# Earlier input rows at the start, and a new place for two output weight pieces and the mix rows, in a two-layer hybrid decoder trunk

## The chip, the cores and the metric

The kernel runs on one core of a Trainium2 chip. The metric is the time of one execution on the device in microseconds; the median of several runs is compared. Engines are called as in the profile: PE is TensorE's matmul, PEld its weight load, DVE is VectorE, ACT is ScalarE, POOL is GpSimd, SP is SyncE, which issues nearly all DMAs here (SPq in the rows).

## The reference

The input x is 2048 rows of 1024 float32. Two layers follow, each `x <- x + RMSNorm_post(mixer(RMSNorm_pre(x)))`. Cut to what matters:

```
def even_mixer(h, w_in, w_out):              # layer 0
    rq, rk, rv, rg, sq, sk, sv, sg = split_cols(h @ w_in, EVEN_SIZES)
    ret = rms_norm(retention(rq, rk, rv)) * silu(rg)        # 4 heads
    sb = stick_breaking(sq, sk, sv) * silu(sg)              # 8 heads
    return concat([ret, sb]) @ w_out                        # 1024 x 1024

def odd_mixer(h, w_in, w_out, ...):          # layer 1
    hq, hf, hi, hg, lx, lg = split_cols(h @ w_in, ODD_SIZES)
    hc = rms_norm(hgrn2(hq, hf, hi, lb)) * silu(hg)         # 4 heads, a gated recurrence
    hl = rg_lru(causal_conv(lx)) * silu(lg)                 # 512 channels, an associative scan
    return concat([hc, hl]) @ w_out                         # 1024 x 1024
```

## The kernel before, in words

The sequence is done in two halves of 1024 rows, so there are four rounds: layer 0 half 0, layer 0 half 1, layer 1 half 0, layer 1 half 1. A round is a mixer (`stick` for layer 0, `hgrn` for layer 1) followed by `out_phase`, the output projection, the post norm and the residual. While `out_phase` works, it also normalises and transposes the rows of the next round (`prep_rows`, `prep_cols`).

**Matmuls.** Every float32 operand of a large matmul is split into a high part (a rounded copy) and a low part (the remainder), and a product is three matmuls: high by high, high by low, low by high. `load_w` (lines 118 to 133) does this for weights: a DMA into a `raw` buffer (pool `wr`, two buffers of 4 KB a partition), a cast on ACT for the high part (L131), a subtraction on DVE for the low part (L132). `proj` (140) is one input projection: 128 output columns, two groups of 512 rows, 24 matmuls a group (L152). Its weights lie in pool `w`, two buffers.

**Start.** The identity for transposes and the two rows of `pre_norm_w` are loaded first (lines 50 to 54), then the eight rows of x of the first half (`row`, L94; a row here is a block of 128 rows) go through a square on ACT (L97), a reciprocal root on DVE and POOL (L70, L71) and a scaling on DVE (L99). After the fourth and the eighth row `step` (106) transposes a group on PE (L112) and makes its high and low part with `pre_norm_w` as a scale (L114 on ACT, L115 on DVE). The first two weight pieces are loaded behind rows 3 and 5 (L127).

**Layer 0.** `stick` opens nine pools, some 114 KB a partition, makes a constant `past` in PSUM from a scratch tile `build` (lines 375 to 379: memset, select on POOL, copy on ACT), and then weaves attention units with the projections and the retention. At its end `ret_gate` (287) projects the gates of heads 2 and 3 alone; each uses a 2 KB `sg` buffer of the two in pool `stmp` for a sigmoid (L296) that L297 reads. The retention's scratch (`srt`) lies behind them and is done earlier.

**Layer 1.** `hgrn` opens the recurrence's pools first (line 789): `lru1`, about 20 KB of scratch (a block-diagonal weight `bd` and four rows of 1024 elements), `lru5`, the four recurrence outputs `ht`, and `lrug`, one 2 KB gate tile `gt`. Behind them lie the pools of the four recurrent heads. `lx_proj(j)` fills `ht` j by a scan (L761); `lg_proj(j)` (769) projects the gates, multiplies by `ht` on POOL (on DVE for the last j; L777) and stores to DRAM, and the last j writes its part of the mix directly (`mix_direct`, L218 and L219). The last weave (934) runs the last head's scan beside the four `lg_proj`.

**Output projection.** `out_phase` (577) opens its pools over the mixer's: `w2` (four weight pieces with high and low part, 32 KB), `o2` (two buffers for rows of the mix), `o1` (post norm weights), `y` (results), then the next round's rows. A weight piece is two of the eight 128-row blocks of `w_out` by 512 columns (`piece`, 592); four pieces make the first 512 columns, four the second. `mix_rows` (221) loads 128 rows of the mix from DRAM (L225) and splits them into the buffers that held the mixer's input (L227 on ACT, L228 on DVE). PE then does 24 matmuls (L640) for each of eight row blocks, twice. `EARLY = (0, 1)` says how many mix row blocks are loaded ahead of `out_phase`, inside the last `lg_proj`, into a `raw` buffer (line 773): none in layer 0, one in layer 1.

**What sets the order.** The tile framework orders the instructions of each engine when the program is built, by the order of the text and its own estimate of when each is ready; each engine then runs its list in order. `tc.high_priority(offset=300)` moves a block 300 places ahead. Pools are stacked from the left end of SBUF, a pool with `side="right"` from the right end; a tile whose place was another tile's waits for that tile's last reader. `weave` and `mixed` interleave two generators by the times that they yield.

Of the kernel before, what the change touches and what calls it, by code (L numbers as in the profile page):

```python
# [9 lines left out]
F32 = mybir.dt.float32  # L10
# [3 lines left out]
ALU = mybir.AluOpType  # L14
# [8 lines left out]
EPS = 1e-6  # L23
LAG = 2
SHIFT = 1
EARLY = (0, 1)
LEVELS = (2, 4, 8, 16, 32, 64)


# [1 line left out]
def tile_trunk(ctx: ExitStack, tc: tile.TileContext, a: dict, out: bass.AP):  # L31
    nc = tc.nc
    x_in = a["x"][0]
    w_in = (a["even_w_in"][0], a["odd_w_in"][0])
    w_out = (a["even_w_out"][0], a["odd_w_out"][0])
# [4 lines left out]
    w_p = ctx.enter_context(tc.tile_pool(name="w", bufs=2))  # L40
# [7 lines left out]
        return (o_bank[-1] if tag == "o" else ps_p).tile([128, 512], F32, tag=tag, name=tag)  # L48

    ident = const.tile([128, 128], F32, name="ident")  # L50
    nc.sync.dma_start(out=ident, in_=a["c_ident"])
    pre_w = const.tile([128, 2, KD], F32, name="pre_w")
    for i in range(2):
        nc.sync.dma_start(out=pre_w[:, i, :], in_=a["pre_norm_w"][i].rearrange("(k p) -> p k", p=128))
    mhalf = const.tile([128, 4], F32, name="mhalf")
    nc.vector.memset(mhalf, -0.5)
    state = const.tile([128, 512], F32, name="state")
# [16 lines left out]
    def scope(es, name, bufs, **kw):  # L74
        return es.enter_context(tc.tile_pool(name=name, bufs=bufs, reuse_waits="tile", **kw))
# [61 lines left out]
    def proj_w(layer, col):  # L137
        ready[layer, col] = load_w(w_in[layer][:, col:col + 128], KD, 128)
# [54 lines left out]
    def weave(*args):  # L193
        run(mixed(*args))
# [175 lines left out]
    def stick(half, xT, M):  # L370
        with ExitStack() as es:
            kv_p, qr_p, q_p, a_p, b_p, wt_p, g_p, t_p, r_p = (scope(es, n, b) for n, b in (
                ("skv", 8), ("sqr", 2), ("sq", 2), ("sa", 6), ("sb", 9), ("swt", 3), ("sg", 3), ("stmp", 2), ("srt", 1)))
            past = scope_o(es, 1).tile([128, 512], F32, tag="past", name="past")
            build = t_p.tile([128, 512], F32, tag="sg", name="build")
            nc.vector.memset(build, 0.0)
            nc.gpsimd.affine_select(out=build[:, 384:512], in_=build[:, 384:512], compare_op=ALU.is_gt, fill=1.0,
                                    base=0, pattern=[[-1, 128]], channel_multiplier=1)
            nc.scalar.copy(out=past, in_=build)
            D_ = [({}, {}, {}, {}) for _ in range(4)]  # L380

            def pair_proj(pr):
# [169 lines left out]
            t_att = 65000 if half else 23000  # L552
            cs = rope_tables(half, r_p)
            run(pair_proj(0))
            flush()
            def qk(*parts):
                return ret_proj_qk(half, xT, r_p, t_p, cs, parts)
# [16 lines left out]
            weave(att(3), t_att, seq(side((5, 8), proj_of(1, pair_gate(3))), gate(0, 1)), 43500)  # L574
            run(gate(2, 3))

    def out_phase(layer, half, M, following):
        prep_row = prep_step = xT = None
        with ExitStack() as es:
            scope_o(es, 2)  # L580
            w2_p, p2, p1, y_p = scope(es, "w2", 4), scope(es, "o2", 2), scope(es, "o1", 1), scope(es, "y", 8)
            if following:
                rows, prep_row, x_p = prep_rows(es, *following)
                xT, prep_step = prep_cols(rows, following[0])
# [2 lines left out]
            early = EARLY[layer]  # L587
            mrs = [None] * early
            mh, ml = zip(*(mix_slot(M, g) for g in range(2)))
            order = (0, 1, 2, 4, 5, 6, 7, 3) if layer == 0 else tuple(range(8))  # L590

            def piece(c, q, pool):
                return load_w(w_out[layer][:, c * 512:(c + 1) * 512], 2, 512, pool, order[2 * q:2 * q + 2])

            with tc.high_priority(offset=300):
                W = [[piece(0, q, w2_p) for q in range(4)], []]
            with tc.high_priority(offset=300):
                for tt in range(early, 8):
                    mrs.append(mix_rows(half, M, tt, p2, "mr"))
# [25 lines left out]
            for c in range(2):  # L625
                if c == 1:
                    if not prep_step:
                        xrs.update((tt, load_x(tt)) for tt in range(8))
                    W[1] += [piece(1, q, w2_p) for q in (2, 3)]
                for tt in range(8):  # L630
                    if (c, tt) == (0, 2):
                        with tc.issue_after(mrs[5]):
                            W[1] += [piece(1, q, w_p) for q in (0, 1)]
# [150 lines left out]

        return lx_proj, lg_proj

    def hgrn(es, half, xT, M):
        scope_o(es, 2)
        lp1, lp5, lpg = scope(es, "lru1", 1), scope(es, "lru5", 4), scope(es, "lrug", 1)
        p1, p, p4 = scope(es, "hg1", 1), scope(es, "hg", 2), scope(es, "hg4", 4)  # L790
        ones = p1.tile([128, 128], F32, name="ones")
        nc.vector.memset(ones, 1.0)
# [138 lines left out]
        flush()  # L931
        for h in range(3):
            weave(head_scan(h), 20000, seq(head_proj(h + 1), lx_proj(h + 1)), 57000)
        weave(head_scan(3), 20000, seq(*(lg_proj(j) for j in range(4))), 41600)
        flush()

    steps = [(layer, half) for layer in range(2) for half in range(2)]
    with ExitStack() as es:
        rows, row, _ = prep_rows(es, 0, 0, 8)
        xT, step = prep_cols(rows, 0)  # L940
        for tt in range(8):
            row(tt)
            if tt in (3, 5):
                proj_w(0, 2048 if tt == 3 else 2560)
            if tt % 4 == 3:
                for k in range(KD):
                    step(tt // 4, k)
    for n, (layer, half) in enumerate(steps):
        M = {}
        if layer == 0:  # L950
            stick(half, xT, M)
            if half == 1:
                nc.vector.memset(state, 0.0)
                odd_const()
        else:
            with ExitStack() as es:
                hgrn(es, half, xT, M)
        xT = out_phase(layer, half, M, steps[n + 1] if n + 1 < len(steps) else None)


def _tables():
# [49 lines left out]
```

## Time and profile before

| | us |
|---|---|
| median of 3 runs | 2286.71 (2285.96 to 2290.03) |
| the profiled execution, its own time | 2291.48 |
| its span, first to last instruction | 2289.6 |
| mean granted clock of TensorE | 0.994 of 2.4 GHz |

In the rows below, a group line gives busy time, mean duration in ns, and the idle time of the engine just before, with what ended most of it. A timeline line is: start, duration, engine, source line, operation, output <- inputs, form, count, and in brackets the idle time before it and its releaser. Line numbers are those of the kernel before.

### The profile page before, as it was taken

How to read it: one execution, taken by the hardware profiler on the slowest of the kernel's cores; microseconds unless marked ns; L12 is line 12 of the kernel's file. 1: busy time of each engine (PE TensorE's matmuls, PEld its weight loads, DVE VectorE, ACT ScalarE, POOL GpSimd, SP SyncE). 2: the span in 40 equal slices, each digit the busy share in tenths (PEclk: the TensorE clock that was granted, in tenths of full speed). 3: DMA queues.
4: the chain of work that ended last, by engine and by line, in shares of the span. 5: the costliest groups of instructions: out<-in, count | busy, mean ns of one | idle time of the engine just before them, and what ended most of it. 6: DMA issues, size and time to landing. Idle time of an engine off the chain costs nothing.

```text
span 2289.6 us, 31620 instructions
## 1 busy us (share of the span) xinstructions
PE 2213.7 (97%) x11392; PEld 1805.6 (79%) x11392; DVE 1390.7 (61%) x2049; ACT 1099.4 (48%) x2192; POOL 706.0 (31%) x992
## 2 busy tenths in 40 slices
PE   7999999999999999999999999999999999999998
PEld 6888877777888888788777887877877877878777
DVE  5545567674567677888898554655555535455543
ACT  5334456553455666777776433243245323433331
POOL 0322244421044344665664001222240013122300
PEclk9999999999999999999999999999999999999999
DMA  6443334246433222213323641111116511111161
GB/s 191 112 124 97 111 104 120 86 132 208 160 103 104 65 74 79 79 50 91 88 58 103 213 151 38 42 38 37 52 50 212 190 47 33 42 37 42 51 221 74
DMA packets 236092, 223.69 MB, mean 98 GB/s; under 512 B 21280, under 2 KB 181408, under 8 KB 235936
## 3 DMA queue, kind: packets, MB, share of 16 engines
q1 hardware_dynamic: 235776, 221.15, 31.4%
q8 instruction: 90, 1.47, 0.3%
q14 instruction: 66, 0.54, 0.1%
q0 software_dynamic: 160, 0.52, 0.1%
HBM read 148.22 MB, written 52.43 MB: 88 GB/s over the span
## 4 chain that ended last, share of the span: by engine, by line
PE 78%; DVE 10%; ACT 4%; DMA 3%; issue 3%; POOL 2%; SPq 0%; POOLq 0%; DVEq 0%; ACTq 0%
PE pp L152 42%; PE pp L640 5%; PE o L640 4%; PE o L515 4%; PE z L640 4%; PE tr L500 4%; PE z L474 2%; DVE a L487 2%; PE z L473 2%; PE z L894 2%; PE tr L112 1%; DMA xr<-in_x 1%; PE z L747 1%; DVE wl L132 1%; DVE wtl L505 1%
## 5 line engine op out<-in xcount | busy, mean ns | idle before, releaser
L152 PE MATMUL pp<-xh,wh 128*128 128x512 f32 x1664 | 687.5, 413 | 0.6 <-ACT xh L114 0.6
L152 PE MATMUL pp<-xh,wl 128*128 128x512 f32 x1664 | 658.1, 396 | 0.0
L152 PE MATMUL pp<-xl,wh 128*128 128x512 f32 x1664 | 656.5, 395 | 0.0
L152 PEld LDWEIGHTS pp<-xh,wl 128*128 128x128 f32 x1664 | 313.4, 188 | 67.7 <-issue 1.4
L490 POOL TENSOR_TENSOR b<-b,a 128x511 f32<-128x511 f32 (+2 forms) x320 | 316.2, 988 | 161.9 <-DVE a L487 96.1
L152 PEld LDWEIGHTS pp<-xh,wh 128*128 128x128 f32 x1664 | 314.3, 189 | 53.9 <-ACT xh L114 1.0
L152 PEld LDWEIGHTS pp<-xl,wh 128*128 128x128 f32 x1664 | 315.1, 189 | 49.3 <-issue 0.5
L487 DVE TENSOR_TENSOR_SCAN a<-a,past 128x512 f32<-128x512 f32 x192 | 244.5, 1275 | 76.6 <-ACT a L477 74.4
L477 ACT ACTIVATE a<-z 128x512 f32<-128x512 f32 (+2 forms) x320 | 172.4, 539 | 235.7 <-PE z L474 197.1
L132 DVE TENSOR_TENSOR wl<-raw,wh 128x1024 fp32r<-128x1024 f32 x136 | 171.1, 1264 | 141.9 <-ACT wh L131 139.6
L131 ACT CAST wh<-raw 128x1024 fp32r<-128x1024 f32 x136 | 142.8, 1053 | 194.1 <-PE pp L152 168.2
L71 POOL TENSOR_TENSOR rs<-rs,mhalf 128x1 f32<-128x1 f32 (+1 forms) x96 | 67.0, 698 | 515.3 <-DVE rs L70 506.6
L505 DVE TENSOR_TENSOR wtl<-tr,wth 128x512 fp32r<-128x512 f32 (+1 forms) x320 | 190.1, 595 | 39.0 <-ACT wth L504 38.0
L504 ACT CAST wth<-tr 128x512 fp32r<-128x512 f32 (+1 forms) x320 | 169.5, 530 | 62.9 <-PE tr L500 61.0
L500 PE MATMUL tr<-ident,b 128*128 128x128 f32 x1088 | 176.1, 276 | 11.8 <-DVE wtl L505 10.7
L500 PEld LDWEIGHTS tr<-ident,b 128*128 128x128 f32 x1088 | 133.5, 141 | 59.1 <-DVE wtl L505 17.6
L478 ACT ACTIVATE b<-z 128x512 f32<-128x512 f32 (+2 forms) x320 | 171.0, 534 | 0.0
L482 DVE TENSOR_TENSOR_SCAN a<-a,past 128x128 f32<-128x128 f32 (+3 forms) x128 | 104.5, 817 | 85.0 <-ACT a L477 84.6
L515 PE MATMUL o<-wth,v 128*128 128x512 f32 (+1 forms) x320 | 128.1, 400 | 0.2 <-ACT mol L521 0.2
L866 POOL TENSOR_TENSOR kg<-kg,t 128x256 f32<-128x256 f32 x96 | 71.1, 740 | 173.2 <-PE z L894 108.0
L480 POOL TENSOR_SCALAR_AFFINE_SELECT b<-b 128x128 f32<-128x128 f32 x128 | 44.2, 345 | 259.6 <-ACT b L478 251.2
L473 PE MATMUL z<-k,qh 128*128 128x512 f32 (+2 forms) x320 | 118.6, 371 | 1.3 <-DMA k<-kd 0.6
(216 smaller groups left out, 3610.3 us busy)
## 6 DMA issues: line engine op xcount, KB each, us to landing
raw<-in_even_w_in SPq DMA_DIRECT2D x56, 512.0 KB, 3.9
raw<-in_odd_w_in SPq DMA_DIRECT2D x48, 512.0 KB, 3.8
xr<-in_x SPq DMA_DIRECT2D x32, 512.0 KB, 4.2
xr<-x1d SPq DMA_DIRECT2D x32, 512.0 KB, 4.5
mr<-mixd SPq DMA_DIRECT2D x32, 448.0 KB, 4.8
qh<-qrh SPq DMA_DIRECT2D x64, 128.0 KB, 2.3
ql<-qrl SPq DMA_DIRECT2D x64, 128.0 KB, 2.4
x1d<-y SPq DMA_DIRECT2D x16, 512.0 KB, 2.9
```

Of the source, the lines that this page charges most:

```text
L132: nc.vector.tensor_tensor(out=wl, in0=raw, in1=wh.bitcast(F32), op=ALU.subtract)
L152: nc.tensor.matmul(ps, w[:, k, :], xx[g][:, k, :], start=(n == 0), stop=(n == 3 * KD - 1))
L473: nc.tensor.matmul(z[:, 0:n], qh[:, tcol], K[e, c][:, 0:n], start=True, stop=False)
L477: nc.scalar.activation(out=A[:, 0:n], in_=z[:, 0:n], func=AF.Sigmoid, scale=-0.125)
L478: nc.scalar.activation(out=B[:, 0:n], in_=z[:, 0:n], func=AF.Sigmoid, scale=0.125)
L487: nc.vector.tensor_tensor_scan(out=A[:, ::-1], data0=A[:, ::-1], data1=past[:, 0:1].to_broadcast([128, 512]), initial=carry[ti][:, 0:1], o ...
L490: nc.gpsimd.tensor_tensor(out=B[:, 0:n - 1], in0=B[:, 0:n - 1], in1=A[:, 1:n], op=ALU.mult)
L500: nc.tensor.transpose(tr[:, ti * 128:ti * 128 + 128], bt[ti][:, sj * 128:sj * 128 + 128], ident)
L504: nc.scalar.copy(out=wh[:, cols], in_=tr[:, cols])
L505: nc.vector.tensor_tensor(out=wl[:, cols], in0=tr[:, cols], in1=wh[:, cols].bitcast(F32), op=ALU.subtract)
L515: nc.tensor.matmul(O[:, cols], V[e, c][:, sj, :], w[:, cols], start=(diag and sj == 0 and w is wh), stop=(c == 0 and sj == 3 and w is wl))
L640: nc.tensor.matmul(ps, m[g][:, k, o:o + 128], w[:, k % 2, :], start=(n == 0), stop=(n == 3 * KD - 1))
```

## The change

The identity's load moves behind the first row of x, the two `pre_norm_w` loads behind the fourth, ahead of the first weight piece. `past` is made after the first pair's projections instead of before. `EARLY` becomes `(0, 0)`, so no mix row block goes through a `raw` buffer. In layer 1 the recurrence scratch `lru1` is placed at the right end and given up after the third `lg_proj`; the last `lg_proj`'s weights are loaded, then a pool `w2a` (two pieces with high and low part, 16 KB) is opened at the right end, and pieces 0 and 1 of `w_out` are loaded there, ahead of the last `lg_proj`. In layer 0 the same pool is opened at the right end when `out_phase` begins. `o2`, the mix rows' buffers, becomes the first pool from the left, and `w2` shrinks to pieces 2 and 3. The pieces 2 and 3 of the second 512 columns take the place of pieces 0 and 1 in `w2a`.

```diff
-EARLY = (0, 1)
+EARLY = (0, 0)
...
-    nc.sync.dma_start(out=ident, in_=a["c_ident"])
...
-    for i in range(2):
-        nc.sync.dma_start(out=pre_w[:, i, :], in_=a["pre_norm_w"][i].rearrange("(k p) -> p k", p=128))
...
-            build = t_p.tile([128, 512], F32, tag="sg", name="build")
...
-            nc.scalar.copy(out=past, in_=build)
...
             run(pair_proj(0))
+            build = t_p.tile([128, 512], F32, tag="sg", name="build")
...
+            nc.scalar.copy(out=past, in_=build)
             flush()
...
+    class first_pieces:
+        def __init__(self, layer, es, instead=None):
+            self.layer, self.es, self.instead = layer, es, instead
+
+        def __iter__(self):
+            if self.instead:
+                proj_w(1, 2560 + 3 * 128)
+                self.instead.close()
+            self.pool = scope(self.es, "w2a", 2, side="right")
+            self.made = [piece(self.layer, 0, q, self.pool) for q in range(2)]
+            return iter(())
+
-    def out_phase(layer, half, M, following):
+    def out_phase(layer, half, M, following, ahead, first):
...
-            w2_p, p2, p1, y_p = scope(es, "w2", 4), scope(es, "o2", 2), scope(es, "o1", 1), scope(es, "y", 8)
+            p2, w2_p, p1, y_p = scope(es, "o2", 2), scope(es, "w2", 2), scope(es, "o1", 1), scope(es, "y", 8)
...
+            if not first:
+                first = first_pieces(layer, ahead)
+                with tc.high_priority(offset=300):
+                    iter(first)
             with tc.high_priority(offset=300):
-                W = [[piece(0, q, w2_p) for q in range(4)], []]
+                W = [first.made + [piece(layer, 0, q, w2_p) for q in (2, 3)], []]
...
-                    W[1] += [piece(1, q, w2_p) for q in (2, 3)]
+                    W[1] += [piece(layer, 1, q, first.pool) for q in (2, 3)]
...
-        lp1, lp5, lpg = scope(es, "lru1", 1), scope(es, "lru5", 4), scope(es, "lrug", 1)
+        scratch = ExitStack()
+        lp1, lp5, lpg = scope(scratch, "lru1", 1, side="right"), scope(es, "lru5", 4), scope(es, "lrug", 1)
...
-        weave(head_scan(3), 20000, seq(*(lg_proj(j) for j in range(4))), 41600)
+        pieces = first_pieces(1, ahead, scratch)
+        weave(head_scan(3), 20000, seq(*(lg_proj(j) for j in range(3)), pieces, lg_proj(3)), 41600)
...
             row(tt)
+            if tt == 0:
+                nc.sync.dma_start(out=ident, in_=a["c_ident"])
+            if tt == 3:
+                for i in range(2):
+                    nc.sync.dma_start(out=pre_w[:, i, :], in_=a["pre_norm_w"][i].rearrange("(k p) -> p k", p=128))
```

## Rows read from the trace of the kernel before

**Rows 1.** The page, part 1: busy us, share of the span, instructions.
```profile
PE 2213.7 (97%) x11392; PEld 1805.6 (79%) x11392; DVE 1390.7 (61%) x2049; ACT 1099.4 (48%) x2192; POOL 706.0 (31%) x992
```
**Rows 2.** PE's waits, whole span: total us, times, longest us.
```profile
PE pp L640 <- ACT wh L131: 5.5, 4, 1.9
...
PE pp L640 <- DVE wl L132: 4.1, 5, 1.2
```
**Rows 3.** Windows: length; PE, PEld, DVE, ACT, POOL busy (count); clock, DMA share, GB/s.
```profile
1719.30:1734.87 15.57, 10.08 (x28) 7.03 (x28) 9.08 (x10) 7.75 (x10) 0.00 (x0) 0.78 0.62 199
2188.39:2201.64 13.25, 9.14 (x28) 6.09 (x28) 7.80 (x8) 7.03 (x9) 0.00 (x0) 0.87 0.67 214
```
**Rows 4.** The chain of waits near the end: start, us, what.
```profile
2212.04 5.44 PE pp L640 x24
```
**Rows 5.** Lines L51, L54, L94: issue in ns, first and last start, landing.
```profile
L51 SPq DMA_DIRECT2D ident<-in_c_ident x1: 395/395/395, 0.8 to 0.8; - x1
...
DMA to landing us min/median/max: 1.8/1.8/1.8
...
L54 SPq DMA_DIRECT2D pre_w<-in_pre_norm_w x2: 423/502/582, 1.3 to 1.7; - x2
...
DMA to landing us min/median/max: 2.4/2.7/2.9
...
L94 SPq DMA_DIRECT2D xr<-in_x x1: 591/591/591, 2.3 to 2.3; - x1
...
DMA to landing us min/median/max: 4.2/4.2/4.2
```
**Rows 6.** Timeline of the start, ACT and PE.
```profile
7.87 1.06 ACT L97 ACTIVATE xn<-xr 128x1024 f32<-128x1024 f32 x1
...
10.20 0.58 ACT L379 COPY past<-build 128x512 f32<-128x512 f32 x1
...
12.24 1.04 ACT L131 CAST wh<-raw 128x1024 fp32r<-128x1024 f32 x1 [0.38 <-DMA raw<-in_even_w_in]
...
14.32 1.26 ACT L114 ACTIVATE xh<-tr,pre_w 128x512 fp32r<-128x512 f32 x2 [1.04 <-DMA xr<-in_x]
...
15.06 0.80 PE L152 MATMUL pp<-xh,wh 128*128 128x512 f32 x1 [0.56 <-ACT xh L114]
```
**Rows 7.** Timeline, layer 1 half 0, before the hand-over: DVE, SP, ACT.
```profile
1675.39 2.34 DVE L761 TENSOR_TENSOR_SCAN ht<-lx,lru_h,ig 128x1024 f32<-128x1024 f32 x1
...
1703.28 0.60 SPq L127 DMA_DIRECT2D raw<-in_odd_w_out  x1
...
1717.26 0.38 SPq L127 DMA_DIRECT2D raw<-in_odd_w_out  x1
...
1719.99 1.04 ACT L131 CAST wh<-raw 128x1024 fp32r<-128x1024 f32 x1
```
**Rows 8.** The chain of waits at the hand-over, layer 1 half 0: start, us, what.
```profile
1719.50 0.61 ACT sg L198
...
1720.85 0.70 DVE gt L777
...
1722.71 3.66 DMA raw<-in_odd_w_out
...
1727.47 1.24 DVE wl L132
```
**Rows 9.** Lines L777 and L132, 1650 to 1722 us: ns min/median/max, first and last start.
```profile
L777 POOL TENSOR_TENSOR gt<-gt,ht x6: 1265/1286/3262, 1660.3 to 1706.3; 128x512 f32<-128x512 f32 x6
...
L132 DVE TENSOR_TENSOR wl<-raw,wh x4: 1220/1225/2007, 1651.7 to 1721.5; 128x1024 fp32r<-128x1024 f32 x4
```
**Rows 10.** Timeline, the hand-over of layer 0 half 0: DVE and PE.
```profile
499.94 0.69 DVE L297 TENSOR_TENSOR ro<-ro,sg 128x512 f32<-128x512 f32 x1 [1.85 <-ACT sg L296]
...
505.11 0.50 PE L640 MATMUL pp<-wh,mh 128*128 128x512 f32 x1 [0.40 <-ACT mh L227]
...
507.70 0.69 DVE L297 TENSOR_TENSOR ro<-ro,sg 128x512 f32<-128x512 f32 x1
```

More of the change, by code (lines that the diff above doesn't have):

```diff
@@ L374, in stick @@
             past = scope_o(es, 1).tile([128, 512], F32, tag="past", name="past")
-            build = t_p.tile([128, 512], F32, tag="sg", name="build")
-            nc.vector.memset(build, 0.0)
-            nc.gpsimd.affine_select(out=build[:, 384:512], in_=build[:, 384:512], compare_op=ALU.is_gt, fill=1.0,
-                                    base=0, pattern=[[-1, 128]], channel_multiplier=1)
-            nc.scalar.copy(out=past, in_=build)
             D_ = [({}, {}, {}, {}) for _ in range(4)]
@@ L554, in stick @@
             run(pair_proj(0))
+            build = t_p.tile([128, 512], F32, tag="sg", name="build")
+            nc.vector.memset(build, 0.0)
+            nc.gpsimd.affine_select(out=build[:, 384:512], in_=build[:, 384:512], compare_op=ALU.is_gt, fill=1.0,
+                                    base=0, pattern=[[-1, 128]], channel_multiplier=1)
+            nc.scalar.copy(out=past, in_=build)
             flush()
@@ L575, in stick, with piece @@
             run(gate(2, 3))
-    def out_phase(layer, half, M, following):
+    def piece(layer, c, q, pool):
+        order = (0, 1, 2, 4, 5, 6, 7, 3) if layer == 0 else tuple(range(8))
+        return load_w(w_out[layer][:, c * 512:(c + 1) * 512], 2, 512, pool, order[2 * q:2 * q + 2])
+    class first_pieces:
[9 more added lines that the diff above has]
+    def out_phase(layer, half, M, following, ahead, first):
         prep_row = prep_step = xT = None
@@ L589, in out_phase @@
             mh, ml = zip(*(mix_slot(M, g) for g in range(2)))
-            order = (0, 1, 2, 4, 5, 6, 7, 3) if layer == 0 else tuple(range(8))
-            def piece(c, q, pool):
-                return load_w(w_out[layer][:, c * 512:(c + 1) * 512], 2, 512, pool, order[2 * q:2 * q + 2])
+            if not first:
+                first = first_pieces(layer, ahead)
+                with tc.high_priority(offset=300):
+                    iter(first)
             with tc.high_priority(offset=300):
-                W = [[piece(0, q, w2_p) for q in range(4)], []]
+                W = [first.made + [piece(layer, 0, q, w2_p) for q in (2, 3)], []]
             with tc.high_priority(offset=300):
@@ L632, in out_phase @@
                         with tc.issue_after(mrs[5]):
-                            W[1] += [piece(1, q, w_p) for q in (0, 1)]
+                            W[1] += [piece(layer, 1, q, w_p) for q in (0, 1)]
                     g, o = tt // 4, (tt % 4) * 128
@@ L785, in lru, with hgrn @@
         return lx_proj, lg_proj
-    def hgrn(es, half, xT, M):
+    def hgrn(es, half, xT, M, ahead):
         scope_o(es, 2)
-        lp1, lp5, lpg = scope(es, "lru1", 1), scope(es, "lru5", 4), scope(es, "lrug", 1)
+        scratch = ExitStack()
+        lp1, lp5, lpg = scope(scratch, "lru1", 1, side="right"), scope(es, "lru5", 4), scope(es, "lrug", 1)
         p1, p, p4 = scope(es, "hg1", 1), scope(es, "hg", 2), scope(es, "hg4", 4)
@@ L933, in hgrn @@
             weave(head_scan(h), 20000, seq(head_proj(h + 1), lx_proj(h + 1)), 57000)
-        weave(head_scan(3), 20000, seq(*(lg_proj(j) for j in range(4))), 41600)
+        pieces = first_pieces(1, ahead, scratch)
+        weave(head_scan(3), 20000, seq(*(lg_proj(j) for j in range(3)), pieces, lg_proj(3)), 41600)
         flush()
+        return pieces
     steps = [(layer, half) for layer in range(2) for half in range(2)]
@@ L949, in tile_trunk @@
         M = {}
+        ahead, first = ExitStack(), None
         if layer == 0:
@@ L956, in tile_trunk @@
             with ExitStack() as es:
-                hgrn(es, half, xT, M)
-        xT = out_phase(layer, half, M, steps[n + 1] if n + 1 < len(steps) else None)
+                first = hgrn(es, half, xT, M, ahead)
+        with ahead:
+            xT = out_phase(layer, half, M, steps[n + 1] if n + 1 < len(steps) else None, ahead, first)
 def _tables():
```

## The prediction

> **What bounds the kernel now.** I read the page's busy shares first: TensorE (PE) is busy 97% of the span [rows 1], so time can only come out of PE's idle stretches and out of stretches at its lower clock. PE's waits come next [rows 2]: matmuls of an output projection (L640) wait for a weight piece's high part (ACT, L131) and low part (DVE, L132). Beside them the change touches the start, where PE's first full matmul begins at 15.06 us [rows 6]. Where the L640 waits lie is seen by asking for PE's busy time in a window at each hand-over from mixer to output projection. Two windows stand out, both in the second layer [rows 3]: from the end of the last input projection, 15.57 us hold 28 matmuls, the first of them begun before, at a mean granted clock of 0.78, and in the second half 13.25 us hold as many at 0.87. A row of 24 such matmuls takes 5.44 us when nothing waits [rows 4], 0.227 each, so 27 new ones take 6.1 us: **9.4 us are lost in one hand-over and 7.1 in the other**, waits and the stretch at 1.2 GHz together (0.78 means 2 x 0.22 x 15.57 = 6.9 us at half of 2.4 GHz).
>
> **Sum to be corrected.** The profiled execution took 2291.48 us (span 2289.6); the median of the runs is 2286.71, so this execution is 4.8 us slow. I subtract savings found in the profile from the median.
>
> **Part 1, the start.** Row 0 of x is issued at 2.35 us and lands 4.2 later; the two pre_w loads in front of it, each a scatter of 4-byte elements, land at 1.3 + 2.4 and 1.7 + 2.9 = 3.7 and 4.6 [rows 5]. So the queue gives a landing every 1.0 us for them, and row 0 follows 1.9 after the second. The change issues row 0 first (1.54 us sooner by issue time alone: 2.35 against 0.81), the identity behind it and pre_w behind row 3. Bounds for row 0: 1.5 us sooner if its 4.2 us stay, 2.7 if it lands at the identity's old landing (0.8 + 1.8) plus its own 1.3 (ACT squares row 1 at 7.87, 1.3 after row 0's landing [rows 6]); I take 2.4, nearest to the second because the queue ahead of it is then empty. (The Trainium skill, "DMA: Bandwidth & Descriptors", section Bandwidth, gives about 10.5 ns for each of 64 packets as the floor of a small transfer; an estimate by it is 0.67 us per pre_w load instead of the 1.0 that the landings show, and row 0 would gain some 0.7 us less. The row stands.)
> The squares on ACT then all start 2.4 sooner, and the copy of `past`, which sits between the squares of rows 2 and 3 with 0.58 us, moves behind the first pair's projections. But the first full matmul at 15.06 also needs the first weight piece, whose cast starts at 12.24 when it lands, 5.7 after row 0, and takes 1.04. With row 0 at 4.15 and the two pre_w loads' 2.0 now between, it lands at 11.85; if those loads only fill gaps, at 9.85. I take 11.5, near the first, since the rows showed the pre_w loads to hold the queue. Cast to 12.6, then the first xh tile (0.63 + 0.1): first matmul near 13.3. **1.8 us**, with ends 0.3 (weight no sooner, ACT busy with xh) and 2.9 (all of 2.4 and 0.5 of the copy) [rows 6]. PE is the fullest engine from there on, so this is kept. The moved pieces (memset, select, copy, about 1.4 us on three engines) are costed at nothing: their first reader is the scan of the first attention unit, and ahead of it lie the first pair's 144 projection matmuls (33 us at 0.227), which leave ACT waiting for PE; if that cover failed, 0.6 us of ACT per half would show.
>
> **Part 2, second layer.** Before, the lookahead of one mix row block takes one of the two `raw` buffers, waits on SyncE for a store, and holds the buffer until its low part is made; so the first weight piece is issued at 1703.28 and the second not before 1717.26 [rows 7]. The chain of waits [rows 8] shows the rest: after PE's last projection, gate sigmoid, two multiplies, then low parts, then a 3.66 us load of the third piece that got its buffer only then, its cast and its subtraction. The change frees the 20 KB of recurrence scratch after its last scan, which ends at 1677.7 [rows 7], puts the hi and lo parts of pieces 0 and 1 there, and drops the lookahead, so both `raw` buffers are free for weights once the last projection's weights are split, before that projection starts. Pieces 0 and 1 are then split while PE still projects, and the loads of pieces 2 and 3 are out of the way too. Rows of the mix come through their own two 3.5 KB buffers, now over the first two recurrence outputs, which the first two gates read, two projections before the end.
> What is late next: the low part of piece 2. By the pools' sizes it lies over the end of the fourth recurrence output and over the gate tile, which the end of the last projection still uses. The new chain, from rows: sigmoid 0.61 from 1719.50, two multiplies of 0.70 (L204 and L777, of one shape), cast into the mix 0.61 and its remainder 0.70 (like the sigmoid and multiply of the same 128x512), low part 1.24, some 0.1 between: done at 1724.15. PE reaches it after 13 matmuls, 1719.30 + 13 x 0.227 = 1722.25. **Residual wait 1.9 us per half.** Piece 3's low part follows 1.24 later, PE needs it six matmuls (1.36 us) later: no further wait. So the halves gain 9.4 - 1.9 = **7.5** and 7.1 - 1.9 = **5.2**. Ends per half: no residual at all, if the compiler's schedule lets the next row block's first 12 matmuls (2.7 us) go in between, and a residual of 4.5 if a wait of this size still brings the half-clock stretch or the order on DVE puts a mix row (about 1 us) first.
> The moved work is 2 casts (1.04) and 2 subtractions (1.24) per half, into a stretch where ACT and DVE wait for PE anyway. The rows warn of one thing: a subtraction that ran beside a POOL multiply took 2.01 instead of its usual 1.22 us, and a multiply there 3.26 against 1.29 [rows 9]. That costs nothing as long as no PE wait hangs on POOL; otherwise see rival B. (The Trainium skill, "SBUF — State Buffer", section Who interferes with whom, says that a VectorE instruction with two SBUF inputs and a GpSimd instruction reading SBUF exclude each other, the later one blocking. The trace agrees in direction: 2.01 and 3.26.)
>
> **Part 3, first layer.** Pieces 0 and 1 go to the right end there too, over rotary scratch, done long before. By the addresses of the kernel before, the right-hand 16 KB begin 128 bytes inside the second 2 KB gate buffer, so piece 0's high part waits for the gate of head 3, group 0. That is read at 499.94 + 0.69; cast 1.04 and low part 1.24 end at about 503, and PE starts there at 505.11, waiting for a mix row and not for weights [rows 10]. Cost nothing, 2 us of cover in hand; gain nothing either. In the second half mix row block 0 now lies over the scratch of the small constants and is issued behind their last use; its cast waits for PE to leave the buffer that it fills, so I cost it nothing, and 0.4, the wait in rows 10, if it is late.
>
> **Sum:** 1.8 + 7.5 + 5.2 = 14.5; 2286.7 - 14.5 = **2272.2 us**.
>
> **Rivals.**
> (B) The moved work collides or comes late. Each of four subtractions delays a POOL multiply by up to 2.0 us [rows 9], and PE's score matmuls in that stretch hang on POOL's products; or the residual is 4.5. Price up to 8 or 5: the gain is about 6.5 to 9.5, **2277 to 2280**. For it: the one measured collision lies in this very stretch. Against: PE has projection matmuls to fill with, and lost little at that collision.
> (C) Slower: the wait in the first layer falls on the wrong tile. The two gate buffers alternate, and which takes the last sigmoid depends on the order of all earlier tiles. If it is the second, piece 0's cast starts only after the last gate product (507.70 + 0.69 = 508.4 [rows 10]), so PE waits from 505.1 to 509.4 and 1.2 more for the low part, 5.5, and loses about 3 more at half clock as it does in the second layer: 8.5 per half, 17 for both. 2286.7 + 17 - 14.5 = **2289.2**, and 2296 with the small ends of parts 1 and 2. It decides once both halves flip; one alone still leaves 2281. Against: the number of tiles before is unchanged.
> (D) The change does not do what it says: the schedule keeps the casts behind the last sigmoid, as it did with piece 0, issued at 1703.28 and cast at 1719.99 [rows 7]. Then one load is spared per half, and the start: **2282**.
>
> **How the numbers follow.** Chances: forecast 0.72 (own range 2267 to 2277), B 0.16, D 0.07, C 0.05. 0.2% is 4.6 us, about what a measurement here can tell from none: faster is below 2282.1. That takes the forecast, B and over half of D less some mishap: 0.88; within: 0.08; slower, most of C: 0.04. The range starts where no residual is left and the start gives 2.9 (2286.7 - 19.4 = 2267.3, a little lower for the scatter of runs) and reaches through B towards D: 2266.5 to 2281.
>
> **What would show it.** Right: the first L152 matmul near 13.3; raw loads of odd_w_out issued before 1700 and two casts L131 ahead of the last sigmoid; the two windows with about 8 us for 27 matmuls and a granted clock of 1.00; the first wait of L640 there being a low part. Wrong: L640 waiting in the first layer for wh (C); longer L777 or L866 with PE waits on them (B); casts still behind the sigmoid (D).

## The result, and the profile after

The change made the kernel slower. The median went from 2286.97 us (2285.96 to 2290.03) to 2309.11 us (2307.82 to 2311.66); the ratio is 1.0097, 95% interval 1.0082 to 1.0112. The profiled execution took 2308.79 us, its span is 2307.0. The forecast was 2272.2, range 2266.5 to 2281.0.

PE's busy time hardly moves. The page of the changed kernel, part 1, answers to [rows 1]:

```profile
PE 2217.5 (96%) x11392; PEld 1804.9 (78%) x11392; DVE 1397.3 (61%) x2049; ACT 1101.1 (48%) x2192; POOL 706.4 (31%) x992
```

PE's waits answer to [rows 2] (total us, times, longest). The output matmul is now L652, the cast of a weight piece L128, the cast of a mix row block L224. The low parts are gone from the top of the list; in their place stand high parts and, new, the mix rows:

```profile
PE pp L652 <- ACT wh L128: 13.2, 4, 5.3
...
PE pp L652 <- ACT mh L224: 11.0, 2, 5.5
```

Where they lie is read as in [rows 3]: a window from the end of the mixer's last projection matmul to the start of the 28th output matmul, here for all four rounds (layer 0 halves 0 and 1, layer 1 halves 0 and 1). Columns: length; busy time of PE, PEld, DVE, ACT, POOL with counts; granted clock; DMA share; GB/s.

```profile
502.02:516.76 14.74, 8.50 (x28) 5.89 (x28) 10.90 (x12) 9.27 (x12) 0.00 (x0) 0.88 0.77 223
1264.00:1280.69 16.69, 9.57 (x28) 6.85 (x28) 11.59 (x14) 9.59 (x12) 0.00 (x0) 0.80 0.74 216
1734.19:1749.88 15.69, 9.22 (x29) 6.79 (x29) 8.72 (x9) 6.97 (x9) 0.00 (x0) 0.78 0.47 145
2203.31:2217.84 14.53, 8.91 (x29) 6.63 (x29) 8.07 (x9) 6.98 (x9) 0.00 (x0) 0.77 0.43 132
```

The same windows of the kernel before, first layer; its second layer is [rows 3]:

```profile
504.55:512.06 7.51, 6.71 (x28) 5.10 (x28) 5.22 (x7) 3.87 (x6) 0.00 (x0) 1.00 0.50 160
1260.21:1266.33 6.12, 6.12 (x29) 5.07 (x28) 5.92 (x7) 4.02 (x6) 0.00 (x0) 1.00 0.45 130
```

27 matmuls at 0.227 are 6.1 us. Before, the four hand-overs lost 1.4, 0, 9.4 and 7.1 us; after, 8.6, 10.6, 9.6 and 8.4. The first layer, costed at nothing, lost 17.8 more, and the second gained nothing. Over the whole output projections (start of the mixer's last projection matmul to the start of the last output matmul) the difference is the whole result. Before, they take 93.4, 89.8, 99.3 and 94.2 us; in the changed kernel (length, PE's busy time, clock, DMA share, GB/s):

```profile
501.79:601.50 99.71, 93.47 (x410) 0.98 0.58 186
1263.77:1365.40 101.63, 94.51 (x410) 0.97 0.57 186
1733.96:1834.60 100.64, 94.17 (x410) 0.97 0.56 189
2203.08:2299.80 96.72, 91.10 (x385) 0.96 0.39 140
```

The lengths add up to 376.8 and 398.7 us: 21.9 more, against 22.1 between the medians. What lies outside them, the mixers and the start, costs about the same as before.

### The profile page after: what moved, and what is told of

The parts are those of the page before. It is cut to its first block, busy times and chain, and to the rows that moved or that the text cites. A ratio compares the mean times of both kernels' runs of the same rounds, so it can differ in the third digit from the quotient of the medians.

```text
span 2307.0 us, 31594 instructions
## 1 busy us (share of the span) xinstructions
PE 2217.5 (96%) x11392; PEld 1804.9 (78%) x11392; DVE 1397.3 (61%) x2049; ACT 1101.1 (48%) x2192; POOL 706.4 (31%) x992
## 4 chain that ended last, share of the span: by engine, by line
PE 80%; DVE 9%; ACT 3%; issue 3%; DMA 2%; POOL 2%; SPq 0%; POOLq 0%; DVEq 0%; ACTq 0%
PE pp L149 42%; PE pp L652 6%; PE o L652 5%; PE z L652 5%; PE o L507 4%; PE tr L492 4%; DVE a L479 2%; PE z L466 2%; PE z L465 2%; PE z L907 2%; DVE wtl L497 1%; PE tr L109 1%; PE z L759 1%; DMA mr<-mixd 1%; DVE wl L129 1%
## 5 line engine op out<-in xcount | busy, mean ns | idle before, releaser
L128 ACT CAST wh<-raw 128x1024 fp32r<-128x1024 f32 x136 | 142.7, 1053 | 186.9 <-PE pp L149 165.5
L507 PE MATMUL o<-wtl,v 128*128 128x512 f32 (+1 forms) x320 | 118.4, 370 | 0.0
```

The lines of the kernel that those rows point to most:

```text
L507: nc.tensor.matmul(O[:, cols], V[e, c][:, sj, :], w[:, cols], start=(diag and sj == 0 and w is wh), stop=(c == 0 and sj == 3 and w is wl))
```

## The experiments

Every kernel was timed beside the kernel before, whose median was between 2286.2 and 2288.7 us in these groups of runs; so two rows are compared by their distance from it. In the table, "projections" is the sum of the four lengths as above, less that of before (376.8); "ratio" is to the kernel before, with its 95% interval. The distance of a median from that of the kernel before beside it and the projections' difference agree within 4 us for each kernel, so the four hand-overs and what follows them are the place to look.

| kernel | median us | ratio | projections |
|---|---|---|---|
| the changed kernel | 2309.11 | 1.0097 (1.0082 to 1.0112) | +21.9 |
| build_back | 2309.23 | 1.0099 (1.0082 to 1.0115) | +24.7 |
| pools_shifted | 2301.55 | 1.0066 (1.0050 to 1.0081) | +11.5 |
| shifted_pad | 2296.17 | 1.0031 (1.0019 to 1.0043) | +6.4 |
| early_mix | 2301.06 | 1.0061 (1.0046 to 1.0075) | +12.4 |
| row_first | 2308.98 | 1.0100 (1.0083 to 1.0116) | +22.5 |
| start_only | 2289.81 | 1.0003 (0.9994 to 1.0011) | +2.5 |
| start_pre_w_later | 2287.37 | 0.9990 (0.9979 to 1.0001) | +1.5 |
| layer0_undone | 2291.23 | 1.0008 (0.9997 to 1.0019) | +2.6 |
| both_mended | 2277.89 | 0.9956 (0.9944 to 0.9967) | -9.5 |
| all_early | 2274.58 | 0.9940 (0.9928 to 0.9952) | -13.8 |
| all_early_old_start | 2272.26 | 0.9927 (0.9914 to 0.9941) | -14.9 |

### The first layer: which overlap, and how it costs

The changed kernel's timeline at the first hand-over shows the cast of piece 0 (with that of piece 1, x2) behind the last sigmoid (L293 at 504.00), behind the fourth mix row block (L224 at 505.02), and begun as the product that reads that sigmoid (L294) ends:

```profile
504.00 0.59 ACT L293 ACTIVATE sg<-pp 128x512 f32<-128x512 f32 x1
505.02 0.94 ACT L224 CAST mh<-mr 128x896 fp32r<-128x896 f32 x1 [0.43 <-DMA mr<-mixd]
...
505.13 0.69 DVE L294 TENSOR_TENSOR ro<-ro,sg 128x512 f32<-128x512 f32 x1
...
505.86 1.99 ACT L128 CAST wh<-raw 128x1024 fp32r<-128x1024 f32 x2
...
506.95 0.52 PE L652 MATMUL pp<-wh,mh 128*128 128x512 f32 x1 [4.77 <-ACT wh L128]
```

That is the place and the order that the prediction's rival C describes, and the built program agrees: the last sigmoid has gone to the second gate buffer. The moved line that makes `past` takes one of these buffers, so it was the suspect. `build_back` puts it back:

```diff
             past = scope_o(es, 1).tile([128, 512], F32, tag="past", name="past")
+            build = t_p.tile([128, 512], F32, tag="sg", name="build")
...
             run(pair_proj(0))
-            build = t_p.tile([128, 512], F32, tag="sg", name="build")
...
```

> The changed kernel with the making of `past` (build) put back ahead of the first pair's projections. Theory T1 (buffer parity): moving it shifted every later use of the two 2 KB gate buffers by one, so that the last sigmoid of the first layer takes the second buffer, whose last 128 bytes lie under piece 0's high part; with build back, the last sigmoid is in the first buffer, both PE waits for wh in the first layer (4.77 + 1.35 and 5.26 + 1.86 us) and the stretch at half clock behind them go: about 6 + 12 = 18 us, 2291 us. Rival R1 (the new place of the pieces costs this by itself: queue of casts, raw buffers): the waits stay and the time is 2309.

Measured: 2309.23, no change. In the built program the last sigmoid is back in the first buffer, which piece 0 does not touch, and yet the order on ACT is what it was:

```profile
504.39 0.59 ACT L293 ACTIVATE sg<-pp 128x512 f32<-128x512 f32 x1
506.03 0.94 ACT L224 CAST mh<-mr 128x896 fp32r<-128x896 f32 x1 [1.04 <-DMA mr<-mixd]
506.87 1.99 ACT L128 CAST wh<-raw 128x1024 fp32r<-128x1024 f32 x2
```

The cast no longer waits for the last product; in the built program its own wait is for head 3, group 0, the tile that the prediction named. It follows the mix row's cast on its own engine, which waits for a load. So the parity theory falls: with piece 0 over the end of the second gate buffer, the instruction order laid down when the program is built has its cast behind the last sigmoid in both programs, whichever of the two buffers that sigmoid takes, and ACT runs in that order. Why the order comes out so was not found. `pools_shifted` takes the overlap itself away, with the parity left flipped:

```diff
-            kv_p, qr_p, q_p, a_p, b_p, wt_p, g_p, t_p, r_p = (scope(es, n, b) for n, b in (
-                ("skv", 8), ("sqr", 2), ("sq", 2), ("sa", 6), ("sb", 9), ("swt", 3), ("sg", 3), ("stmp", 2), ("srt", 1)))
+            kv_p, qr_p, q_p, a_p, b_p, g_p, t_p, wt_p, r_p = (scope(es, n, b) for n, b in (
+                ("skv", 8), ("sqr", 2), ("sq", 2), ("sa", 6), ("sb", 9), ("sg", 3), ("stmp", 2), ("swt", 3), ("srt", 1)))
```

> The changed kernel with the gate buffers opened two pools earlier, so that the right-hand 16 KB lie over rotary scratch and the softmax weights alone; build stays where the change put it, so the parity stays flipped. T1: the overlap is gone, so the first-layer waits go as well, 2291 us. Rival R1b (build's new place does the harm by the order of the work, not by an address): the waits stay, 2309.

Measured: 2301.55, 15.3 us above the kernel before beside it in place of 22.1. In the first half the last weight cast now stands ahead of the last two sigmoids, no wait is left, and the window loses 0.1 us. In the second half the waits for weights are gone too, but there is a new one, for mix rows:

```profile
495.99 1.05 ACT L128 CAST wh<-raw 128x1024 fp32r<-128x1024 f32 x1 [1.13 <-DMA raw<-in_even_w_out]
499.44 0.60 ACT L293 ACTIVATE sg<-pp 128x512 f32<-128x512 f32 x1 [2.40 <-PE pp L149]
...
1257.98 0.16 DVE L724 TENSOR_SCALAR lam<-s 128x4 f32<-128x4 f32 x1
1258.21 1.29 SPq L222 DMA_DIRECT2D mr<-mixd  x2
...
1263.03 0.76 PE L652 MATMUL pp<-wh,mh 128*128 128x512 f32 x1 [3.76 <-ACT mh L224]
```

The first mix row's load is issued when the last of the small constants (L724, on 128x4 elements) is done: their scratch lies under the first mix row buffer. Those are some 35 tiny DVE instructions, interleaved with the gates. They lie there in the changed kernel as well, but cost it nothing: its order has the last of them some 8 us ahead of the last projection matmul (which begins at 1263.77), here 0.7 us ahead of it (1258.88), and its first mix row is cast while PE still projects. The changed kernel:

```profile
1255.26 0.16 DVE L724 TENSOR_SCALAR lam<-s 128x4 f32<-128x4 f32 x1
1259.76 0.94 ACT L224 CAST mh<-mr 128x896 fp32r<-128x896 f32 x1 [4.50 <-DMA mr<-mixd]
```

So moving the pools removed one overlap's cost and, by another order on DVE, brought out a second one's. `shifted_pad` leaves 320 bytes free ahead of the buffer:

```diff
+            if layer == 0:
+                scope(es, "pad", 1).tile([128, 80], F32, name="pad")
             p2, w2_p, p1, y_p = scope(es, "o2", 2), scope(es, "w2", 2), scope(es, "o1", 1), scope(es, "y", 8)
```

> As pools_shifted, and in the first layer 320 bytes are left free ahead of the two mix row buffers, so that the first no longer lies over the scratch of the small constants. Theory T3: what is left of the loss in the first layer (waits of 3.76 and 1.88 us for mix rows in its second half, and some 3 us at half clock behind them) is the first row's load waiting for the last of these constants on VectorE; it goes: 2293 to 2296. Rival: the rows are late by their stores or by the queue, and the time stays at 2301.

Measured: 2296.17, 8.0 us above the kernel before beside it and at the end of what was expected, and the two first-layer windows are nearly those of before:

```profile
505.26:511.95 6.69, 6.51 (x28) 4.99 (x27) 4.75 (x7) 3.02 (x5) 0.00 (x0) 1.00 0.53 161
1262.61:1269.85 7.24, 6.47 (x28) 5.19 (x28) 5.00 (x10) 3.30 (x5) 0.00 (x0) 1.00 0.60 172
```

Without the two overlaps, of 128 and some 300 bytes, 14 of the 22 us are gone, in a layer that had nothing to gain. `layer0_undone` says the same from the other side, with the first layer's pieces and rows where they lay before:

> The changed kernel with only the first layer's output projection put back as it was. Theory T1b: the whole slowdown is the first layer's; the second layer, with two pieces early but no lookahead, loses what it lost before (15.9 and 14.8 us for 28 matmuls against 15.6 and 13.2): 2287 to 2291. Rival: the second layer gained or lost by itself, 2282 or less, or 2295 or more.

Measured: 2291.23, ratio 1.0008, whose interval holds 1: the slowdown is the first layer's, and the second layer as changed neither gained nor lost more than 3 us (its two projections take 99.5 and 96.6 us, before 99.3 and 94.2). Why shifted_pad stays 5 us above layer0_undone was not followed further; half of it lies in the first layer's second projection, 92.3 against 89.8, where the trace has a wait of 0.8 us for the last of the constants.

### The second layer: what the lookahead was worth

After the last projection (its last matmul begins at 1733.96) the changed kernel's timeline goes on like this:

```profile
1734.38 0.60 ACT L195 ACTIVATE sg<-pp 128x512 f32<-128x512 f32 x1 [3.23 <-PE pp L149]
...
1735.74 0.69 DVE L789 TENSOR_TENSOR gt<-gt,ht 128x512 f32<-128x512 f32 x1
...
1736.46 0.62 ACT L215 CAST mh<-gt 128x512 fp32r<-128x512 f32 x1 [1.48 <-DVE gt L789]
1736.99 1.99 ACT L128 CAST wh<-raw 128x1024 fp32r<-128x1024 f32 x2
1738.88 0.93 ACT L224 CAST mh<-mr 128x896 fp32r<-128x896 f32 x1
...
1739.87 0.79 PE L652 MATMUL pp<-wh,mh 128*128 128x512 f32 x1 [5.52 <-ACT mh L224]
```

Pieces 0 and 1 are cast well ahead, as forecast, and the load of the first mix row block is issued before the last sigmoid too:

```profile
1704.04 1.05 ACT L128 CAST wh<-raw 128x1024 fp32r<-128x1024 f32 x1 [1.71 <-PE pp L149]
...
1706.22 1.05 ACT L128 CAST wh<-raw 128x1024 fp32r<-128x1024 f32 x1 [0.64 <-DMA raw<-in_odd_w_out]
...
1722.92 0.56 SPq L222 DMA_DIRECT2D mr<-mixd  x1
```

What PE lacks is the first mix row block. Its load takes 4.4 us, so it lies ready from 1727.3 on; but its cast stands on ACT behind the casts of pieces 2 and 3, and these stand behind the cast of the last product (L215, which waits for L789). Piece 2's high part lies over the fourth recurrence output, which that product reads, in any case. The second block is later still. The chain of waits of the changed kernel (start, us, what) shows its load issued when L789 ends, since its buffer lies over the fourth recurrence output:

```profile
1735.74 0.70 DVE gt L789
...
1736.46 4.56 DMA mr<-mixd
```

`row_first` writes the load and cast of block 0 ahead of pieces 2 and 3 in the program:

```diff
             with tc.high_priority(offset=300):
+                if layer == 1:
+                    mrs.append(mix_rows(half, M, 0, p2, "mr"))
                 W = [first.made + [piece(layer, 0, q, w2_p) for q in (2, 3)], []]
             with tc.high_priority(offset=300):
-                for tt in range(early, 8):
+                for tt in range(len(mrs), 8):
```

> The changed kernel with only the order in the second layer altered: the load and the cast of mix block 0 are written ahead of pieces 2 and 3, in the same buffer. T2: block 0 has landed long before, so its cast runs before the last sigmoid; the wait of 5.5 us becomes one of about 2 for piece 2: 4 to 7 us less per half, 2295 to 2301, about as with the lookahead. Rival R2 (its load, or the buffer over a recurrence output that is read late, is what is late): no gain, 2305 to 2309.

Measured: 2308.98, with the same 11.0 us in two waits for the first mix rows in PE's list. This does not tell the two theories apart: in the built program the order on ACT came out as it was, with block 0's cast behind both pieces. Here the place in the text did not set it. `early_mix` does move it, by restoring the lookahead (`EARLY = (0, 1)` and nothing else):

> The changed kernel with the lookahead of one mix row block in the second layer restored (EARLY = (0, 1)). Theory T2: in the second layer PE waits 5.5 us for the first mix rows, whose cast stands on ACT behind the casts of pieces 2 and 3, and these wait for the last gate product; with block 0 cast before the last sigmoid PE starts at once with pieces 0 and 1, and waits some 2 us for piece 2 instead: 4 to 7 us less per half, 2295 to 2301. Rival R2 (what is late is the loading of mix rows, or the weights): a gain under 2 us per half, 2305 to 2309. The first layer is as in the changed kernel.

Measured: 2301.06, 14.8 us above the kernel before beside it in place of 22.1, so 7 us less, at the upper end of the range that T2 expected. Block 0 is cast between the last two sigmoids, PE runs on, and what it waits for is piece 2:

```profile
1731.61 0.93 ACT L224 CAST mh<-mr 128x896 fp32r<-128x896 f32 x1
...
1736.85 0.40 PE L652 MATMUL pp<-wh,mh 128*128 128x512 f32 x1
...
1740.75 0.50 PE L652 MATMUL pp<-wh,mh 128*128 128x512 f32 x1 [0.94 <-ACT wh L128]
1742.01 0.56 PE L652 MATMUL pp<-wl,mh 128*128 128x512 f32 x1 [0.76 <-DVE wl L129]
```

0.94 + 0.76 = 1.7 us, close to the residual of 1.9 that the prediction took; but the first and longer of the two waits is for piece 2's high part, of which the prediction's chain knew nothing. `both_mended` joins this with the first layer as it was:

> The changed kernel with the first layer's output projection as it was before (four pieces and the mix rows where they lay), and with the lookahead of one mix row block in the second layer. Theories T1b (the first layer lost by the new place of pieces and rows alone, some 20 us) and T2 (the second by the missing lookahead) together: nothing lost in the first layer, and in the second a wait of about 1.7 us and some 1.7 us of half clock per half in place of 9.4 and 7.1 us: 6 + 4 us faster than before, with the start's 0 to 2: 2274 to 2278. Rival: the two parts do not add up, 2283 or more.

Measured: 2277.89, ratio 0.9956. Its two windows of the second layer lose 2.4 and 4.0 us in place of 9.4 and 7.1; the second has a stretch at 1.2 GHz behind the waits, the first has none:

```profile
1714.70:1723.18 8.48, 6.78 (x29) 4.99 (x27) 6.44 (x7) 5.34 (x7) 0.00 (x0) 1.00 0.67 227
2176.66:2186.74 10.08, 8.38 (x29) 6.13 (x27) 6.44 (x7) 5.34 (x7) 0.00 (x0) 0.83 0.68 215
```

### The start

In the changed kernel row 0 is squared at 4.45 instead of 6.58, but the fourth row at 10.36 instead of 10.71, and most of that is the copy of `past`, which stood ahead of it [rows 6]. The kernel before:

```profile
10.71 1.05 ACT L97 ACTIVATE xn<-xr 128x1024 f32<-128x1024 f32 x1
```

The timeline of the changed kernel, ACT, SP and PE:

```profile
3.14 3.30 SPq L962 DMA_DIRECT2D pre_w<-in_pre_norm_w  x2
6.48 3.58 SPq L124 DMA_DIRECT2D raw<-in_even_w_in  x1
...
10.36 1.06 ACT L94 ACTIVATE xn<-xr 128x1024 f32<-128x1024 f32 x1 [0.21 <-DMA xr<-in_x]
...
14.41 0.69 ACT L111 ACTIVATE xh<-tr,pre_w 128x512 fp32r<-128x512 f32 x1 [2.90 <-PE tr L109]
15.00 1.03 ACT L128 CAST wh<-raw 128x1024 fp32r<-128x1024 f32 x1
...
16.71 0.78 PE L149 MATMUL pp<-xh,wh 128*128 128x512 f32 x1
```

The first xh tile needs four rows, and the fourth lands at 10.3 (issued at 2.66, 7.7 us to landing), before at 10.5 (3.93 and 6.5). So the first xh tile comes at 14.41, before at 14.32 [rows 6]: nothing is gained on the rows. The first weight piece is issued at 6.48, because SP sits 2.8 us in the issue of the second pre_w load, and lands 7.3 later at 13.8 instead of 12.2. Its cast now stands on ACT behind the first xh tile, at 15.00, where it was ahead of it at 12.24, and on PE four transposes of a later xh tile stand ahead of the first full matmul, which moves from 15.06 to 16.71. By its landing alone the weight could have been cast before that xh tile was done (13.8 + 1.0 against 15.1): the later landing and the order that the program was built with were not told apart. `start_only` is the kernel before with the new order of loads alone, `start_pre_w_later` has the pre_w loads behind the first weight piece as well:

```diff
             if tt in (3, 5):
                 proj_w(0, 2048 if tt == 3 else 2560)
+            if tt == 3:
+                for i in range(2):
+                    nc.sync.dma_start(out=pre_w[:, i, :], in_=a["pre_norm_w"][i].rearrange("(k p) -> p k", p=128))
```

> The kernel before with the new order of the first loads alone. Theory T4: the first projection needs four rows, and the fourth lands when it did (10.3 against 10.5 us in the traces), while the first weight piece, now behind the two loads of pre_w, lands 1.5 us later: first full matmul near 16.7 instead of 15.06, no gain: 2285 to 2288. Rival (the prediction): 1.8 us faster, 2284.4 or less.

> start_only with the two pre_w loads behind the first weight piece as well. T4: the first weight piece lands near 12.2 again, the fourth row near 10.3 as ever, first full matmul at 15.0 to 15.6 and not 16.8, at most 0.5 us before the kernel before's 15.06, so nothing that the time can tell: 2284 to 2289. Rival: the rows, no longer followed by pre_w, land sooner and the first full matmul comes by 14.

Measured: 2289.81 and 2287.37, ratios 1.0003 and 0.9990: neither can be told from no change (start_only lies 1.8 us above the range expected). The place of pre_w does what T4 says, and no more: the first full matmul begins at 16.78 in start_only and at 15.16 in start_pre_w_later. The timeline of `start_pre_w_later`:

```profile
12.14 1.05 ACT L128 CAST wh<-raw 128x1024 fp32r<-128x1024 f32 x1 [0.43 <-DMA raw<-in_even_w_in]
...
15.16 0.80 PE L149 MATMUL pp<-xh,wh 128*128 128x512 f32 x1 [0.56 <-ACT xh L111]
```

### A version that beats both

If nothing of the hand-over is to wait for the last gate, all four pieces and both mix row buffers must lie over scratch that dies earlier. The per-head tiles of the second layer have four buffers, two for each of two heads in flight; those of the even heads are dead once head 2 is scanned. `all_early` gives them a pool of their own next to `lru1`, 20 KB more, and leaves the first layer as it was:

```diff
-        p1, p, p4 = scope(es, "hg1", 1), scope(es, "hg", 2), scope(es, "hg4", 4)
+        p1, p = scope(es, "hg1", 1), scope(es, "hg", 2)
+        p4s = (scope(scratch, "hg4", 2, side="right"), scope(es, "hg5", 2))
...
+            p4 = p4s[h % 2]
...
-            self.pool = scope(self.es, "w2a", 2, side="right")
-            self.made = [piece(self.layer, 0, q, self.pool) for q in range(2)]
+            self.pool = scope(self.es, "w2a", 4, side="right")
+            self.rows = scope(self.es, "o2", 2, side="right")
+            self.made = [piece(self.layer, 0, q, self.pool) for q in range(4)]
```

> As both_mended without the lookahead, but in the second layer a further 20 KB is given up early: the per-head tiles of even heads have a pool of their own, and all four weight pieces and the two mix row buffers lie over scratch that is dead before the last projection. By T2 and the order of ACT nothing of the hand-over then waits for the last gate: both losses of the second layer go, 9.4 + 7.1: 2269 to 2272. Rival: the mix rows are still cast late, or the moved subtractions collide with GpSimd's products: 2276 or more.

Measured: 2274.58, ratio 0.9940. The two windows of the second layer lose 0.2 us each, at full clock:

```profile
1717.48:1723.77 6.29, 6.29 (x29) 5.06 (x27) 4.51 (x6) 3.00 (x4) 0.00 (x0) 1.00 0.62 180
2177.70:2183.99 6.29, 6.29 (x28) 5.07 (x27) 4.28 (x6) 3.00 (x4) 0.00 (x0) 1.00 0.52 159
```

That is 13.6 us below the 2288.21 of the kernel before in the runs beside it, 3 short of the 16.5 at stake and 2.6 above the range expected; the later parts of the second layer's projections give that much back (they are 12.8 us shorter in all, their windows above 16.2), which was not followed further. With the old order of the first loads:

> all_early with the order of the first loads put back as it was. Theory T4 (the start's change gives nothing): the same as all_early within 2 us, 2273 to 2277. Rival (the prediction's part 1): 1.8 us slower than all_early.

Measured: 2272.26, ratio 0.9927, 2.3 us below all_early (2.8 measured from the kernel before beside each), with intervals that overlap: no sign of the gain that the start's order was forecast to give.

## Why the prediction was wrong

**Part 3, the step that failed most.** "Piece 0's high part waits for the gate of head 3, group 0 ... Cost nothing, 2 us of cover in hand." Measured: 7.2 and 10.6 us more at the two hand-overs. The working took a cast to run as soon as its data and its place are free. On ACT it runs where the built order has it, and over the gate buffers that was behind the last sigmoid and the mix rows, with both `raw` buffers held meanwhile (piece 2 could be issued only at 508.84, and PE waited 1.35 for it at 514.81). Rival C had the place, the first wait and a price of 17 us right, at a chance of 0.05; its condition, which of two buffers comes last, was wrong, and with it the reason for its price: `build_back` shows that either will do. So its agreement with 17.8 is in part luck, and so is its second wait, which it took for piece 0's low part. The argument against it did not hold either: the number of tiles was unchanged, and still the moved line changed which buffer the last sigmoid takes.

**Part 3, second half.** "its cast waits for PE ... so I cost it nothing, and 0.4 ... if it is late." In the changed kernel this came out: the first mix row is cast 4 us before the last projection matmul begins. What the place can cost shows in another order alone: 3.76 + 1.88 us of waits in pools_shifted, and 7.4 us less above the kernel before in shifted_pad.

**Part 2.** Early pieces: right, two casts of L128 before 1707. The residual for piece 2: 1.7 against 1.9, and with the clock 2.4 to 4.0 lost, within the ends given (0 to 4.5); the size is right, the chain only in part, since the first wait is for a high part and not for the low part that was named as a sign. Wrong: dropping the lookahead was booked as a gain, two free `raw` buffers, and never as a loss. The sentence was "Rows of the mix come through their own two 3.5 KB buffers, now over the first two recurrence outputs, which the first two gates read". The second buffer lies over the fourth output, read last, and the first row's cast is queued behind two casts that wait for the last gate. The question "what is late next" was put to the weights alone. The term of 12.7 became a loss of about 1.5 (9.6 + 8.4 against 9.4 + 7.1).

**Part 1.** 1.8 us, ends 0.3 to 2.9; measured a first matmul 1.65 us later, and nothing in the time. Failed: "The squares on ACT then all start 2.4 sooner." Row 0's started 2.1 sooner, the next three 0.1 to 0.4. The fourth row, which the first tile needs, was issued 1.3 us sooner and landed 0.1 sooner (10.34 against 10.46), and the weight behind pre_w came at 13.8, not 11.5. The weight lands 3.4 us after the fourth row, against 1.75 before: put down to the two pre_w loads, 0.8 each instead of 1.0. But they land only 0.35 and 0.40 us apart behind that row (10.34, 10.69, 11.09), and the weight's issue was held up as well, so what one such load costs is not shown. The Trainium skill, "DMA: Bandwidth & Descriptors", section Bandwidth, gives a floor per packet of a small transfer, from which the estimate was 0.67 each; this trace, with 0.4 by the landings and 0.8 by the weight, does not decide between it and the 1.0.

**Moved `past`**: nothing, as costed. Rival B: collisions of DVE and POOL did occur (one of the moved subtractions took 2.31 us at 1707.53, beside a POOL product at 1707.24), but its price did not show: no wait of PE on L789 or on POOL stands near the hand-overs. Rival D did not come about either, the casts did move.

The sum failed by 17.8 us in part 3, 14.2 in part 2 and about 2 in part 1, 34 of the 37 between 2272.2 and 2309.1; 2.6 more lie in the output projections behind the 28th matmul.

## What to carry to other kernels

An overlap of 128 bytes was enough here to put a cast behind the last use of a pool's buffers, though in build_back the one tile under it was free some 5 us sooner; when a pool moves, list every pool under it with its last use, and give scratch that dies late the places that are taken late. Each engine here runs its instructions in the order of the built program, so a wait on one tile delays all that stands behind it: read the order on ACT in the built program, not only what each instruction needs, and read it again after each mend, since a mend can bring out another overlap (pools_shifted). Before a lookahead is dropped, ask what its work covered.

## What the runs showed that was not expected

The same stretch at the same work ran at different clocks in the traces of different kernels, which the change does not explain: from 255 to 275 us the granted clock is 0.91 in before, all_early and start_only, and 1.00 in the changed kernel, both_mended, all_early_old_start and layer0_undone. In the traces of before and of the changed kernel PE waits 2.11 us near 263 us (L361 at 262.38 before, L358 at 263.25 after), and in the 20 us around it PE is busy for the same 17.89 us, but gets 94 matmuls done in the one and 104 in the other. The kernel before (length, PE's busy time, clock, DMA share, GB/s):

```profile
255.00:275.00 20.00, 17.89 (x94) 0.91 0.45 132
```

The changed kernel:

```profile
255.00:275.00 20.00, 17.89 (x104) 1.00 0.45 132
```

At 0.91, 3.6 of the 20 us are at 1.2 GHz and some 1.8 us of work are lost. In the four windows of the changed kernel, with waits of 4.8 to 5.5 us, the granted clock is 0.77 to 0.88; behind the same waits of 0.94 and 0.76 us it was 1.00 in one of both_mended's windows and 0.83 in the other. A few such stretches more or fewer would be of the size by which executions of one kernel differ here (13 us among 23 of the kernel before); that they are the cause was not shown. A hand-over is better judged by its window than by the time of one execution.
